# Where a second input piece is issued: SyncE's third load moves to ScalarE's queue, and its transposes are split among the matmuls

## The chip, the cores and the metric

The kernel runs on one core of a Trainium2 chip. The metric is device time in microseconds (us). Three runs of the kernel before gave 117.21, 117.22 and 117.49 us; their median is 117.22 us. A profile is taken in an execution of its own, and its times are counted from the start of its span.

## What is computed

```python
# a: 1024 x 1024, b: 1024 x 2048, c: 2048 x 1024, all float32
h = np.matmul(a, b)
h = 0.5 * h * (1 + np.tanh(np.sqrt(2 / np.pi) * (h + 0.044715 * h ** 3)))
return np.matmul(h, c).astype(np.float32)
```

## The kernel before, in words

TensorE contracts over the partition dimension, so the kernel builds `aT`, the transpose of a in bf16, and computes h transposed: a matmul takes 128 columns of b as weights and 512 columns of `aT` as the moving side. a is handled in eight pieces (h, q): h is the half of its rows (512), q the quarter of its columns (256). A piece becomes two of the eight k-tiles of `aT[:, h]`. b's first 512 columns are loaded in k-tiles of 128 rows; they are multiplied plainly (`mm1`, `block`). The rest of h, and the product with c, is done by class `Seven`, which replaces eight block products by seven and needs sums and differences of blocks on VectorE; that begins at about 24.9 us and is not touched.

The change lies in the first 11 us. What sets the order there:

- **Loads in float32 by SyncE (SP).** `sta` holds pieces of a, `stb` k-tiles of b. Five loads are issued one after the other: a(0,0) at L75, b's k-tiles 0 and 1 at L76 (512 KB, called b0 below), a(1,0) at L77, a(0,1) at L78, b's k-tile 2 at L79. None of them waits for anything.
- **Loads that cast to bf16, by GpSimd (POOL).** Everything else is loaded by GpSimd's queue, straight into `abq` (the five remaining pieces of a, 256 KB each as written), `b1`, `b2` and `c_sb`. The first of them stands behind `gate` (L81), a one-element copy out of a(0,0): no cast-load is issued before a(0,0) has landed. The last piece of a, a(1,3), is the seventh and last of the L86/L89 loads.
- **Casts.** `cast_a` copies a landed piece to bf16 (`ab`), parts of it on VectorE (L110) and ScalarE (L108); `cast_b` does so for a k-tile of b. For a(1,0) VectorE casts the columns of the first k-tile and ScalarE those of the second.
- **Turns.** `turn` is a generator with two steps. Each does four 128 x 128 transposes on TensorE into a PSUM bank (L145) and copies the bank to `aT` on VectorE (L146); `next(tn)` runs one step. Where the steps stand among the matmuls is written out by hand.
- **Matmuls.** `block(h, tiles, ks)` issues, for each k and each tile of 128 columns of b, one matmul of 512 columns (L114).

ScalarE's first instruction is a GELU of one column, `g` (L82). It is there for the table load that it brings, and is called the warm-up. `stir` (L122) gives TensorE work while it waits for the first data.

The stretch that the change edits (L236 to L242) casts b's k-tile 1 and a(1,0), runs four matmuls on k-tile 0 and two on k-tile 1, then both steps of a(1,0)'s turn, then the last two matmuls on k-tile 1. After it come the casts of a(0,1) (L243), three matmuls with a(1,0) (L248) and the turn of a(0,1) (L249), called turn(0,1) below. The turn of the last piece, turn(1,3), stands at L274.

The kernel's functions as they stand before the change:

Of the kernel before, what the change touches and what calls it, by code (L numbers as in the profile page):

```python
# [19 lines left out]
def kernel(ctx, tc, a, b, c, out):  # L20
    nc = tc.nc
    M, K = a.shape
    _, N = b.shape
    _, P = c.shape
# [15 lines left out]
    def slot(tag, shape, dt, name):  # L40
        return big.tile(shape, dt, name=name, tag=tag)

    def bank(i, shape=(128, H), dt=F32, name="ps"):
        return pp.tile(list(shape), dt, name=name, tag=f"bank{i}", padded_shape=None)
# [21 lines left out]
    sta = slot("x1", [128, 2, 2, 4, 256], F32, "sta")  # L66
    abq = slot("x3", [128, 4, 2, 4, 256], BF16, "abq")

    def a_part(h, q):
        return av[:, 4 * h:4 * h + 4, ds(q * 256, 256)]  # L70

    def b_part(q):
        return bv[:, 2 * q:2 * q + 2, 0:H]

    nc.sync.dma_start(out=sta[:, 0, 0], in_=a_part(0, 0))  # L75
    nc.sync.dma_start(out=stb[:, 0:2], in_=b_part(0))  # L76
    nc.sync.dma_start(out=sta[:, 1, 0], in_=a_part(1, 0))  # L77
    nc.sync.dma_start(out=sta[:, 0, 1], in_=a_part(0, 1))  # L78
    nc.sync.dma_start(out=stb[:, 2], in_=bv[:, 2, 0:H])  # L79

    nc.gpsimd.tensor_copy(gate, sta[:, 0, 0, 3, 0:1])  # L81
    nc.scalar.activation(g, warm[:, 0:1], AF.Gelu_apprx_tanh)  # L82


    def cast_load_a(h, q):
# [13 lines left out]
    for n in range(2):  # L99
        for k in range(0, KT, 4):  # L100
            nc.gpsimd.dma_start(out=b2[:, k:k + 4, ts(n, H)],
                                in_=bv[:, k:k + 4, ds(1024 + n * H, H)])
# [9 lines left out]
    def mm1(p, t, h, ks):  # L112
        for k in ks:
            nc.tensor.matmul(p, b1[:, k, ts(t, 128)], aT[:, h, k],  # L114
                             start=(k == 0), stop=(k == KT - 1))
# [12 lines left out]
    def cast_a(h, q, *engs):  # L128

        ab = pieces("ab", 2, [128, 4, 256], BF16, "ab")  # L130
        for i, eng in enumerate(engs):
            w = 256 // len(engs)
            for j, e in enumerate(eng if isinstance(eng, tuple) else (eng,)):
                m = slice(2 * j, 2 * j + 2) if isinstance(eng, tuple) else slice(0, 4)
                copy(e, ab[:, m, ts(i, w)], sta[:, h, q][:, m, ts(i, w)])
        return ab

    def turn(h, q, i, ab):

        banks = i if isinstance(i, tuple) else (i,)  # L140
        pts = [bank(x, (128, 2, H), BF16, "pt") for x in banks]
        for n in range(2):
            pt = pts[n % len(pts)]
            for m in range(4):
                nc.tensor.transpose(pt[:, n, ts(m, 128)], ab[:, m, ts(n, 128)], ident)  # L145
            nc.vector.tensor_copy(aT[:, h, 2 * q + n], pt[:, n])  # L146
            yield
# [8 lines left out]
    def block(h, tiles, ks):  # L156
        for k in ks:
            for t in tiles:
                mm1(ps[h, t], t, h, (k,))
# [70 lines left out]
    tn = turn(0, 0, 4, cast_a(0, 0, nc.vector))  # L230
# [5 lines left out]
    cast_b(1, nc.scalar)  # L236
    ab = cast_a(1, 0, nc.vector, nc.scalar)
    block(0, range(4), (0,))
    block(0, range(2), (1,))
    for _ in turn(1, 0, (7, 6), ab):  # L240
        pass
    block(0, range(2, 4), (1,))  # L242
    ab = cast_a(0, 1, (nc.scalar, nc.vector), nc.vector)  # L243
    cast_b(2, nc.scalar, nc.scalar)
    for t in range(3):
# [3 lines left out]
    tn = turn(0, 1, 7, ab)  # L249
# [4 lines left out]
    for q in range(1, 3):  # L254
        k = 2 * q
        block(0, range(4), (k,))
        tn = turn(1, q, 7, abq[:, q, 1])
# [5 lines left out]
        tn = turn(0, q + 1, 7, abq[:, q + 1, 0])  # L263
# [10 lines left out]
    tn = turn(1, 3, 0, abq[:, 3, 1])  # L274
# [213 lines left out]
```

## Time and profile before

| what | value |
|---|---|
| median of three runs | 117.22 us |
| profiled execution: its own time | 117.6 us |
| profiled execution: its span | 115.8 us |
| TensorE busy | 110.7 us (96% of the span) |
| VectorE, ScalarE, GpSimd busy | 90.1, 51.4, 17.3 us |
| granted TensorE clock | 1.0 in the whole span |
| bytes read from HBM, written | 20.97 MB, 4.19 MB |

The 1.8 us between the profiled execution's time and its span lie outside the recorded work. That execution is 0.4 us above the median, so a difference worked out from its rows is added to 117.22 us.

How it is read: TensorE's busy share is near the span everywhere, and the modelled ends of matmuls make it look closer than it is. What the edited stretch is worth is seen in the order of events between 0.7 and 21.7 us: when each load is issued and lands, when the first instruction that needs it starts, and where TensorE's rows leave a gap. In the half-microsecond windows the last two columns are the mean busy share of the 16 DMA engines and the GB/s written; a cast-load writes half of what it reads.

### The profile page before, as it was taken

To read this page: it belongs to the slowest core of one execution; us is meant where nothing else is said; L and a number is where in the kernel's file an instruction comes from. 1 tells how busy PE (TensorE), PEld (TensorE's weight loads), DVE (VectorE), ACT (ScalarE), POOL (GpSimd) and SP (SyncE) were. 2 spreads that over 40 slices of the span, in tenths; PEclk is the share of its full clock that TensorE was granted. 3 is DMA by queue.
4 is the path that set the end of the run, shared out by engine and by line. 5 is a ranking of instruction groups with operands and counts; after the bars stand their busy time and mean duration, and the time that the engine had idled before them with its cause. 6 is when DMAs were issued, how large, how long until landed. Compare 5 with 4: busy or idle time off the path is not lost.

```text
span 115.8 us, 1473 instructions
## 1 busy us (share of the span) xinstructions
PE 110.7 (96%) x544; PEld 77.1 (67%) x550; DVE 90.1 (78%) x108; ACT 51.4 (44%) x86; POOL 17.3 (15%) x29
## 2 busy tenths in 40 slices
PE   7889999999999999999999999999999999999990
PEld 6545555445777447888886444588888888888870
DVE  0247747689999998944789999999999986964581
ACT  5053000799268998066699339700043992000000
POOL 2497754222332000000000000000000000000000
PEclk9999999999999999999999999999999999999999
DMA  3999999999999999998000000070000002004994
GB/s 74 296 381 221 200 199 204 204 207 207 205 210 210 211 212 212 212 210 163 9 0 0 6 0 0 0 272 0 0 0 0 0 0 94 2 27 173 364 358 166
DMA packets 13414, 15.94 MB, mean 138 GB/s; under 512 B 736, under 2 KB 9184, under 8 KB 13408
## 3 DMA queue, kind: packets, MB, share of 16 engines
q0 software_dynamic: 8672, 9.31, 47.6%
q1 hardware_dynamic: 4592, 6.42, 15.7%
q10 hardware_dynamic: 144, 0.13, 0.3%
q8 instruction: 4, 0.07, 0.2%
q14 instruction: 2, 0.02, 0.0%
HBM read 20.97 MB, written 4.19 MB: 217 GB/s over the span
## 4 chain that ended last, share of the span: by engine, by line
PE 79%; DMA 13%; POOL 5%; issue 0%; DVE 0%
PE ps L212 76%; DMA abq<-in_a_dram 10%; DMA sta<-in_a_dram 3%; POOL abq L86 3%; PE ps L114 2%; POOL b L89 1%; POOL gate L81 1%; PE pt L145 1%; POOL b L92 0%; DVE ot L375 0%
## 5 line engine op out<-in xcount | busy, mean ns | idle before, releaser
L212 PE MATMUL ps<-x,s 128*128 128x512 f32 x128 | 29.6, 391 | 0.0
L212 PEld LDWEIGHTS ps<-x,s 128*128 128x128 f32 x128 | 24.0, 188 | 5.1
L212 PE MATMUL ps<-x,x 128*128 128x512 f32 x96 | 22.9, 394 | 0.0
L212 PEld LDWEIGHTS ps<-x,x 128*128 128x128 f32 x96 | 18.0, 188 | 3.9
L114 PE MATMUL ps<-aT,b 128*128 128x512 bf16 x62 | 15.7, 379 | 0.3 <-DVE b L110 0.2
L298 ACT ACTIVATE v<-ps 128x512 f32<-128x512 f32 x10 | 6.0, 598 | 19.1 <-PE ps L212 19.1
L212 PE MATMUL ps<-c_sb,hT 128*128 128x512 bf16 (+2 forms) x78 | 14.1, 336 | 0.1
L212 PE MATMUL ps<-x 128*128 128x512 f32 x56 | 13.2, 393 | 0.0
L212 PEld LDWEIGHTS ps<-x 128*128 128x128 f32 x56 | 10.2, 188 | 2.7 <-ACT u L298 0.4
L212 PEld LDWEIGHTS <-hT 128*128 128x128 bf16 x80 | 7.1, 98 | 7.0 <-issue 0.5
L118 ACT ACTIVATE hT<-ps 128x512 bf16<-128x512 f32 x14 | 7.3, 596 | 9.6 <-PE ps L114 9.6
L118 ACT ACTIVATE hT<-ot 128x512 bf16<-128x512 f32 x18 | 10.4, 623 | 2.1 <-DVE ot L303 2.0
L146 DVE COPY aT<-pt 128x512 bf16<-128x512 bf16 x16 | 6.7, 422 | 5.5 <-PE pt L145 5.4
L212 PE MATMUL ps<-aT,b 128*128 128x512 bf16 x46 | 10.6, 379 | 0.1
L303 DVE TENSOR_TENSOR ot<-ps,u 128x512 f32<-128x512 f32 x10 | 6.7, 688 | 5.2 <-ACT u L298 5.2
L303 DVE TENSOR_TENSOR ot<-ps,v 128x512 f32<-128x512 f32 x10 | 6.7, 688 | 4.9 <-DMA out_dram<-ot 3.9
L170 DVE TENSOR_TENSOR x<-c_sb 128x1024 fp32r<-128x1024 bf16 x8 | 9.2, 1216 | 0.0
L114 PEld LDWEIGHTS <-b 128*128 128x128 bf16 x64 | 5.7, 97 | 4.5 <-DVE b L110 0.3
L212 PEld LDWEIGHTS <-b 128*128 128x128 bf16 x48 | 4.6, 97 | 5.7 <-issue 0.3
L104 POOL DMA_DIRECT2D c_sb<-in_c_dram x8 | 5.6, 703 | 13.4 <-DMA b<-in_b_dram 11.1
L170 DVE TENSOR_TENSOR x<-b 128x1024 fp32r<-128x1024 bf16 (+1 forms) x4 | 7.0, 1751 | 0.6 <-issue 0.6
L298 ACT ACTIVATE u<-ps 128x512 f32<-128x512 f32 x10 | 5.9, 597 | 3.4 <-PE ps L212 3.2
(44 smaller groups left out, 110.7 us busy)
## 6 DMA issues: line engine op xcount, KB each, us to landing
c_sb<-in_c_dram POOLq DMA_DIRECT2D x8, 512.0 KB, 19.7
out_dram<-ot SPq DMA_DIRECT2D x14, 256.0 KB, 2.1
b<-in_b_dram POOLq DMA_DIRECT2D x6, 512.0 KB, 15.6
sta<-in_a_dram SPq DMA_DIRECT2D x3, 512.0 KB, 6.2
abq<-in_a_dram POOLq DMA_DIRECT2D x5, 256.0 KB, 8.0
stb<-in_b_dram SPq DMA_DIRECT2D x1, 512.0 KB, 5.4
b<-in_b_dram POOLq DMA_DIRECT2D x2, 256.0 KB, 8.3
stb<-in_b_dram SPq DMA_DIRECT2D x1, 256.0 KB, 7.2
```

The source lines that it names most:

```text
L81: nc.gpsimd.tensor_copy(gate, sta[:, 0, 0, 3, 0:1])
L86: nc.gpsimd.dma_start(out=abq[:, q, h], in_=a_part(h, q))
L89: nc.gpsimd.dma_start(out=b1[:, 2 * q:2 * q + 2, 0:H], in_=b_part(q))
L104: nc.gpsimd.dma_start(out=c_sb[:, t:t + 2], in_=cv[:, t:t + 2])
L114: nc.tensor.matmul(p, b1[:, k, ts(t, 128)], aT[:, h, k], start=(k == 0), stop=(k == KT - 1))
L118: nc.scalar.activation(hT[h][:, t], p, AF.Gelu_apprx_tanh)
L145: nc.tensor.transpose(pt[:, n, ts(m, 128)], ab[:, m, ts(n, 128)], ident)
L146: nc.vector.tensor_copy(aT[:, h, 2 * q + n], pt[:, n])
L170: nc.vector.tensor_tensor(out=dst[:, r], in0=x[:, r], in1=y[:, r], op=op)
L212: nc.tensor.matmul(p[:, ds(c0, w)], l[:, k, ts(j, 128)], r[:, k, ds(c0, w)], start=(start and k == 0), stop=(k == self.kt - 1), skip_group ...
L298: nc.scalar.activation(st, p, AF.Copy)
L303: nc.vector.tensor_tensor(out=ot, in0=p, in1=st, op=ADD)
```

## The change

The load of a(1,0) is taken out of SyncE's list and issued from ScalarE's queue, after the warm-up in program order; it has no wait. SyncE's two later loads move up one place. On TensorE, one matmul of k-tile 1 stands ahead of the first step of a(1,0)'s turn instead of two ahead of the whole turn; two follow the first step, and one the second. No instruction is added or removed on any engine.

```diff
     nc.sync.dma_start(out=sta[:, 0, 0], in_=a_part(0, 0))
     nc.sync.dma_start(out=stb[:, 0:2], in_=b_part(0))
-    nc.sync.dma_start(out=sta[:, 1, 0], in_=a_part(1, 0))
     nc.sync.dma_start(out=sta[:, 0, 1], in_=a_part(0, 1))
     nc.sync.dma_start(out=stb[:, 2], in_=bv[:, 2, 0:H])
 
     nc.gpsimd.tensor_copy(gate, sta[:, 0, 0, 3, 0:1])
     nc.scalar.activation(g, warm[:, 0:1], AF.Gelu_apprx_tanh)
+    nc.scalar.dma_start(out=sta[:, 1, 0], in_=a_part(1, 0))
...
     block(0, range(4), (0,))
-    block(0, range(2), (1,))
-    for _ in turn(1, 0, (7, 6), ab):
-        pass
-    block(0, range(2, 4), (1,))
+    block(0, (0,), (1,))
+    tn = turn(1, 0, (7, 6), ab)
+    next(tn)
+    block(0, (1, 2), (1,))
+    next(tn)
+    block(0, (3,), (1,))
     ab = cast_a(0, 1, (nc.scalar, nc.vector), nc.vector)
```

## The prediction

> **What bounds the kernel now.** I read three views in this order: the chain of work that ended last, the timeline of the first 22 us, and half-microsecond windows over the same stretch. The chain first:
>
> ```profile
> 27 pieces in order of time: start us, us, what
> ...
> 0.74 3.70 DMA sta<-in_a_dram
> 4.44 0.05 issue
> 4.49 0.70 POOL gate L81
> ...
> 10.15 11.43 DMA abq<-in_a_dram
> 21.58 0.05 issue
> 21.63 0.40 PE pt L145 x4
> ```
>
> From 21.63 on the chain is TensorE alone, so the end moves one for one with the start of turn(1,3). Two things meet there: the landing of a(1,3) at 21.58, and TensorE itself. The timeline (start, duration, engine, line, operation; what the idle time ended on stands in brackets):
>
> ```profile
> 0.74 0.42 SPq L75 DMA_DIRECT2D sta<-in_a_dram  x1
> 0.74 1.28 ACT L82 ACT_TABLE_LOAD   x1 [0.74 <-PEq L472]
> ...
> 1.22 0.50 SPq L76 DMA_DIRECT2D stb<-in_b_dram  x1
> 1.77 0.46 SPq L77 DMA_DIRECT2D sta<-in_a_dram  x1
> 2.04 0.20 ACT L82 ACTIVATE g<-const-float32-0.0 128x1 f32<-128x1 f32 x1
> ...
> 6.90 1.47 PE L114 MATMUL ps<-aT,b 128*128 128x512 bf16 x6 [0.17 <-DVE b L110]
> ...
> 7.99 0.43 DVE L110 CAST ab<-sta 128x512 bf16<-128x512 f32 x1 [0.68 <-DMA sta<-in_a_dram]
> ...
> 8.47 0.62 PE L145 MATMUL pt<-ident,ab 128*128 128x128 bf16 x8
> ...
> 10.03 0.39 PE L145 MATMUL pt<-ident,ab 128*128 128x128 bf16 x4
> ...
> 19.16 2.32 PE L114 MATMUL ps<-aT,b 128*128 128x512 bf16 x10
> ```
>
> The ten matmuls from 19.16 give the pitch: (2.32 - 0.38) / 9 = 0.215 us, 0.38 being the length of one. TensorE would be ready for turn(1,3) at 19.16 + 10 x 0.215 = 21.31 and starts at 21.63: its **slack is 0.32 us**. Four transposes cost 0.22 (12.02 to the matmul at 12.24). From 10.03 to 21.31 the rows follow at these pitches, so a delay before 10.03 passes through, less 0.32.
>
> The landing at 21.58 is softer than it looks. In the trace's semaphore events fifteen of the sixteen DMA engines had finished a(1,3) by 19.92 and one at 21.58; the packets of the instruction queue (q8 on the page) show a 16 KB packet that starts at 19.57 and takes 0.97 us. I read this as an instruction fetch that came in front of that engine's last packets. Such packets start at 19.57, 40.92, 66.49 and 96.05, 202 to 265 TensorE rows apart, so I take it to follow TensorE's progress. If TensorE is later by over 0.1 us, the fetch should come behind a(1,3), which lands near 20.0, and TensorE alone decides. If TensorE is earlier, the fetch still hits, and an earlier turn(1,3) needs an earlier stream.
>
> **The edit of the order.** After the change TensorE has, from its first real matmul to turn(0,1), 4 + 1 + 2 + 1 + 3 = 11 matmuls and eight transposes: 11 x 0.215 + 2 x 0.22 = 2.81 us if nothing is missing. Before, the same work took 10.03 - 6.90 = 3.13, because a(1,0), landing at 7.97, let the transposes begin at 8.47 only. With unchanged landings the new order is slightly worse: five matmuls end at 7.98 instead of six at 8.19, both before 8.47, so one more stands behind (0.215), and VectorE's copy of the second step (0.42) with the first cast of a(0,1) (0.28) then follow transposes that end near 9.5: turn(0,1) at 10.3, +0.27. That lies within the slack: 21.31 + 0.27 = 21.58 against 21.63. So the order by itself costs nothing; without the slack it would cost 0.27.
>
> **The moved load.** What ScalarE's queue does with a DMA behind an ACTIVATE has no row; two bounds do. Late: after `g`, 2.04 + 0.20 = 2.24. Early: as soon as the queue can pass it, at about 0.85 behind the table load's start at 0.74. I take early. The trace shows ScalarE's sequencer passing the semaphore waits of L202 at 21.09, before the third and fourth GELU ahead of it (21.41, 21.89) have started, and `g` starts 0.01 after the table load ends, as if already queued. Nothing else stands behind this issue (0.42 to 0.71 by SyncE's five rows) on ScalarE until the cast at 6.62.
>
> SyncE's a(0,1) and b's k-tile 2 are issued 0.5 us sooner (one issue with its gap); they lie behind b0 in the same queue, so that buys nothing while the engines are full. GpSimd's queue is moved past nothing, but its gate waits for a(0,0). Then the bytes:
>
> ```profile
> 4.00:4.50 0.50, 0.50 (x4) 0.35 (x2) 0.04 (x1) 0.00 (x0) 0.01 (x1) 1.00 1.19 303
> 4.50:5.00 0.50, 0.29 (x2) 0.00 (x0) 0.50 (x1) 0.00 (x0) 0.50 (x1) 1.00 0.75 221
> 5.00:5.50 0.50, 0.29 (x5) 0.29 (x5) 0.15 (x1) 0.00 (x0) 0.50 (x2) 1.00 0.85 233
> ...
> 7.00:7.50 0.50, 0.50 (x3) 0.29 (x3) 0.31 (x1) 0.50 (x2) 0.50 (x2) 1.00 1.10 387
> ```
>
> The last two columns are the DMA engines' share and GB/s. Full rate is near 387. Adding the windows up, a(0,0)'s 0.524 MB are through at 3.80 (landing 4.44), b0's at 5.71 (landing 6.62, 0.9 later), a(1,0)'s at 7.15 (landing 7.97). The engines are never idle for long, so a(1,0) can only come earlier by taking bytes from a(0,0) and b0, or by filling the dip between 4.0 and 5.75.
>
> Issued early, a(1,0) runs beside a(0,0). Both are through between 5.08 (0.250 MB at 3.0, the rest at 385) and 5.71 (when the first two loads were before). b0 follows: 1.36 us at full rate, 1.91 if its dip moves with it, but no later than 7.15, when the same three loads were through. So b0 lands between 5.08 + 1.36 + 0.9 = 7.34 and 7.15 + 0.9 = 8.05, against 6.62. I take the middle, 7.7, since either end rests on one of two readings of the dip. First matmul 0.28 after the landing as now (6.62 to 6.90): 7.98; turn(0,1) at 7.98 + 2.81 = 10.79, +0.76; less the slack, **+0.44 us**. The ends give +0.08 (7.34) and +0.79 (8.05). a(0,0), landing near 5.6, puts its own turn about 1.1 us later, under the longer wait for b0.
>
> The Trainium skill speaks against the move: "DMA: Bandwidth & Descriptors", section "Issuing engines are not separate DMA queues", says that DMAs of all issuing engines end on the same 16 engines and only the sequencer's issue time is saved. By that rule alone the gain would be the 0.5 us of issue time, hidden, so nothing. The same page, section "Queues, rings and completion order", has each engine take turns between queue rows packet by packet. By that, b0 is pushed back as above; no row here shows two such hardware queues sharing for long, and GpSimd's queue beside SyncE's speaks otherwise, as the second rival says.
>
> **Rivals.**
>
> 1. *The gate becomes the wall.* a(0,0) lands 1.0 to 1.2 us later, and with it GpSimd's issues. Before, they begin at 5.14 and their first packet runs at 8.82 in the trace, just as SyncE's loads run out. If those 3.7 us are latency and not a wait for free engines, the whole cast stream shifts by about 1.0, and so does a(1,3): 118.2. For it: nothing is written by that queue before 8.8. Against: it starts on each engine just when SyncE's packets end there.
> 2. *a(1,0) is served last.* If an engine empties SyncE's queue before another's, as that start at 8.82 suggests, a(1,0) lands at about 9.4, where the four other loads end. Its transposes start 0.5 later at 9.9, turn(0,1) comes after two steps and six matmuls (0.44 + 1.29) at 11.63: +1.60, less 0.32 is +1.28, so 118.5.
> 3. *The other side: the issue is late and fills the dip.* If the DMA does wait for `g`, it is issued at 2.24 and its packets come 1.1 later (0.74 to the first packet at 1.83), at 3.3, when a(0,0) is nearly through. What b0 leaves free between 4.0 and 5.75, (387 - 265) x 1.75 = 0.21 MB or up to 0.5 us, carries a(1,0), which then lands near 7.6 with b0 still near 6.6. First step at 8.08 (cast, as now, 0.5 after landing), turn(0,1) near 9.85 (-0.18), and the stream behind is 0.4 earlier, a(1,3) at 21.2: -0.4, 116.8. It decides if b0 lands before 6.9.
> 4. *It does not do what it says.* The load is taken in the old place between b0 and a(0,1): only the order is left, 117.2.
>
> **How the numbers follow.** About 0.3% (0.35 us) is what a measurement of this kernel can tell from no change. Forecast, 0.44 chance: 117.22 + 0.44 = 117.66, own range 117.3 to 118.0; of it 0.31 beyond 0.35 us and 0.13 within. Gate 0.12, all slower. Served last 0.10, slower. Late and filling 0.22: 0.18 faster, 0.04 within. No effect 0.12, within. Slower 0.53, within 0.29, faster 0.18. The range leaves out rival 2 and the outermost of rival 3: 116.75 to 118.3.
>
> **What would show it.** Right: the issue row of a(1,0) starts before 1.3 with the warm-up still running; a(0,0) lands after 5.2, b0 between 7.3 and 8.1 and not far from a(1,0); first L114 matmul near 8.0, turn(0,1) near 10.8; a(1,3) lands near 20 with no wait ahead of turn(1,3). Wrong: an issue row at 2.2 or later; b0 at 6.6; GpSimd's loads landing a microsecond later with TensorE waiting for `abq`; a wait on a(1,0) before its transposes.

## The result, and the profile after

Eleven runs of the kernel before, taken beside those of the changed one, have a median of 117.33 us; the changed kernel's eleven have 118.70 (117.74 to 119.88). The ratio is 1.0077, 95% interval 1.0050 to 1.0105: slower by 0.9 us. In four of the eleven the mean granted TensorE clock was 0.982 to 0.986; the ratio leaves them out. The forecast was slower, by 0.44 us.

The profiled execution of the changed kernel took 118.7 us with a span of 116.9. Its timeline (start, duration, engine, line, operation, what the idle time ended on):

```profile
0.74 1.28 ACT L81 ACT_TABLE_LOAD   x1 [0.74 <-PEq L474]
...
0.74 0.44 SPq L75 DMA_DIRECT2D sta<-in_a_dram  x1
...
0.80 0.46 ACTq L82 DMA_DIRECT2D sta<-in_a_dram  x1
...
5.18 0.69 DVE L110 CAST ab<-sta 128x1024 bf16<-128x1024 f32 x1 [5.18 <-DMA sta<-in_a_dram]
...
7.66 1.50 PE L114 MATMUL ps<-aT,b 128*128 128x512 bf16 x5 [0.21 <-DVE b L110]
...
10.77 0.38 PE L145 MATMUL pt<-ident,ab 128*128 128x128 bf16 x4
...
13.51 1.04 PE L114 MATMUL ps<-aT,b 128*128 128x512 bf16 x4 [0.38 <-DMA b<-in_b_dram]
...
17.48 0.23 PEld L145 LDWEIGHTS <-abq 128*128 128x128 bf16 x4 [0.50 <-DMA abq<-in_a_dram]
...
22.79 0.39 PE L145 MATMUL pt<-ident,abq 128*128 128x128 bf16 x4
```

The load behind the warm-up does not stand behind it: it is issued at 0.80, while the table load runs. VectorE's first cast starts at 5.18 instead of 4.46, the first matmul on data at 7.66 instead of 6.90, turn(0,1) at 10.77 instead of 10.03. That is 0.72 to 0.76, once. It begins with the order of the packets: b0's first packet runs at 5.00 instead of 3.66, now that a(1,0)'s packets run beside a(0,0)'s and ahead of it, and from there to its landing b0 takes 2.36 us instead of 2.93. Then comes a wait at 13.51 for b's k-tile 3, a cast-load. The kernel before runs the same four matmuls without one:

```profile
12.24 1.03 PE L114 MATMUL ps<-aT,b 128*128 128x512 bf16 x4
```

A second wait, for `abq` at 17.48, grew by 0.20 us (the kernel before has 0.30 there). So turn(1,3) starts at 22.79 instead of 21.63. The chain of waits now runs through that load:

```profile
39 pieces in order of time: start us, us, what
...
5.91 0.81 POOL abq L86
6.72 6.74 DMA b<-in_b_dram
13.47 0.05 issue
13.51 1.04 PE ps L114 x4
```

The windows of the changed kernel at those times (last two columns: share of the DMA engines, GB/s written):

```profile
3.50:4.00 0.50, 0.50 (x3) 0.41 (x2) 0.00 (x0) 0.00 (x0) 0.00 (x0) 1.00 1.09 389
4.00:4.50 0.50, 0.50 (x3) 0.41 (x2) 0.00 (x0) 0.00 (x0) 0.00 (x0) 1.00 1.03 362
...
10.00:10.50 0.50, 0.50 (x4) 0.20 (x2) 0.42 (x2) 0.15 (x1) 0.50 (x2) 1.00 1.47 130
10.50:11.00 0.50, 0.50 (x7) 0.33 (x6) 0.50 (x2) 0.00 (x0) 0.50 (x2) 1.00 0.78 87
11.00:11.50 0.50, 0.50 (x6) 0.26 (x4) 0.48 (x2) 0.00 (x0) 0.50 (x1) 1.00 0.98 73
```

and of the kernel before at two of them:

```profile
10.50:11.00 0.50, 0.50 (x5) 0.23 (x4) 0.38 (x1) 0.32 (x2) 0.48 (x1) 1.00 1.33 205
11.00:11.50 0.50, 0.45 (x6) 0.35 (x6) 0.14 (x1) 0.00 (x0) 0.00 (x0) 1.00 1.32 195
```

From 10 to 12 the cast stream of the changed kernel runs at 73 to 130 GB/s where it ran at about 200. In the trace's packets the reads of k-tile 3 took 96 to 1044 ns in that stretch instead of 96 to 98, and its sixteen parts land between 11.00 and 13.47 (before: 11.29 to 11.98). Some reads of a among them were slow too (mean 204 ns from 11.0 to 11.5, where 60 is usual). This is called the stall below. It is measured by how long after a(1,1), the cast-load ahead of it, k-tile 3 lands: 2.78 us instead of 0.64.

### The profile page after: what moved, and what is told of

Same layout as the page of the kernel before. It is cut to its first block, busy times and chain, and to the rows that moved or that the text cites. A ratio compares the mean times of both kernels' runs of the same rounds, so it can differ in the third digit from the quotient of the medians.

```text
span 116.9 us, 1473 instructions
## 1 busy us (share of the span) xinstructions
PE 111.1 (95%) x544; PEld 77.3 (66%) x550; DVE 89.9 (77%) x108; ACT 51.3 (44%) x86; POOL 17.2 (15%) x29
## 4 chain that ended last, share of the span: by engine, by line
PE 86%; DMA 10%; POOL 1%; issue 0%; DVE 0%
PE ps L212 75%; PE ps L114 9%; DMA b<-in_b_dram 6%; DMA sta<-in_a_dram 4%; PE pt L145 2%; POOL abq L86 1%; POOL gate L80 1%; DVE ot L377 0%
## 5 line engine op out<-in xcount | busy, mean ns | idle before, releaser
L212 PE MATMUL ps<-x 128*128 128x512 f32 x56 | 13.2, 392 | 0.0
L118 ACT ACTIVATE hT<-ot 128x512 bf16<-128x512 f32 x18 | 10.6, 625 | 1.8 <-DVE ot L305 1.7
L212 PE MATMUL ps<-aT,b 128*128 128x512 bf16 x46 | 10.6, 379 | 0.1
```

Source lines behind the costliest of these rows:

```text
L118: nc.scalar.activation(hT[h][:, t], p, AF.Gelu_apprx_tanh)
L212: nc.tensor.matmul(p[:, ds(c0, w)], l[:, k, ts(j, 128)], r[:, k, ds(c0, w)], start=(start and k == 0), stop=(k == self.kt - 1), skip_group ...
```

## The experiments

Theory A (shared start): two hardware queues share the engines from the start, so b0, the third load, is late, and TensorE with it. Theory B: the new order of turns carries the loss. Theory C asks whether the stall in the cast stream belongs to the change (C1) or is chance (C2); later its cause is sought in GpSimd's later issue (G) or in the second hardware queue (Q).

Landings (the last of sixteen parts) are from the semaphore events, starts from the timeline, us; "b0 first" is the start of b0's first packet, and behind k-tile 3's landing stands how long after a(1,1) it came. The ratio has its 95% interval.

| kernel | a(0,0) | a(1,0) | b0 first | b0 | k-tile 3 | first matmul | turn(0,1) | turn(1,3) | span | ratio |
|---|---|---|---|---|---|---|---|---|---|---|
| before | 4.44 | 7.97 | 3.66 | 6.59 | 11.98 (+0.64) | 6.90 | 10.03 | 21.63 | 115.8 | 1 |
| changed | 5.16 | 5.63 | 5.00 | 7.36 | 13.47 (+2.78) | 7.66 | 10.77 | 22.79 | 116.9 | 1.0077 (1.0050-1.0105) |
| order_only | 4.24 | 7.86 | 3.41 | 6.49 | 11.88 (+0.65) | 6.81 | 10.15 | 21.43 | 115.6 | 1.0026 (1.0007-1.0045) |
| move_only | 5.20 | 5.67 | 4.90 | 7.22 | 12.84 (+2.28) | 7.53 | 10.39 | 22.09 | 116.2 | 1.0125 (1.0088-1.0162) |
| late | 4.29 | 10.06 | 3.46 | 6.41 | 12.55 (+1.25) | 6.77 | 12.43 | 23.72 | 117.8 | 1.0202 (1.0183-1.0222) |
| swap | 6.71 | 8.06 | 2.50 | 6.44 | 13.22 (+1.72) | 9.41 | 14.12 | 25.41 | 119.5 | 1.0239 (1.0168-1.0310) |
| before_gate2 | 4.10 | 7.90 | 3.41 | 6.54 | 11.94 (+0.71) | 6.92 | 9.97 | 21.26 | 115.4 | 0.9995 (0.9955-1.0035) |
| after_timed | 5.17 | 5.65 | 4.97 | 7.56 | 11.94 (+0.70) | 7.87 | 10.91 | 22.21 | 116.4 | 1.0079 (1.0037-1.0120) |
| after_b3first | 5.11 | 5.58 | 4.88 | 7.27 | 10.50 (ahead of it) | 7.58 | 10.44 | 21.73 | 115.9 | 1.0057 (1.0011-1.0103) |
| before_later | 4.25 | 8.81 | 3.39 | 7.22 | 13.11 (+0.96) | 7.53 | 10.88 | 22.43 | 116.6 | 1.0075 (1.0047-1.0103) |
| after_earlier | 5.29 | 5.76 | 5.01 | 7.30 | 12.58 (+1.66) | 7.71 | 10.57 | 21.90 | 116.1 | 1.0089 (1.0050-1.0129) |
| one_queue | 4.23 | 6.26 | 4.94 | 9.53 | 13.56 (+0.68) | 10.10 | 14.61 | 25.90 | 120.0 | 1.0352 (1.0313-1.0392) |
| after_stir | 5.28 | 5.76 | 5.01 | 7.54 | 13.07 (+2.19) | 7.85 | 10.90 | 22.40 | 116.6 | 1.0094 (1.0072-1.0116) |

The span is the start of turn(1,3) plus 94.1 to 94.2 us in every row. So all that these profiles differ by within the span happens before it. Where a(1,0) is issued at 0.80 from ScalarE's queue, b0's first packet runs at 4.88 to 5.01; with the old loads and in late it runs at 3.39 to 3.66.

**after_again**: the changed kernel once more, no edit.

> The changed kernel once more. Theory A (shared start): ScalarE's issue starts near 0.8, a(0,0) lands near 5.2, b0 near 7.4, first L114 matmul near 7.7, as in the first profile. Theory C1 (the stall in the cast stream belongs to the change): b's k-tile 3 lands near 13.5 again and TensorE waits about 0.4 us for it near 13.5; ratio 1.007 to 1.011. Theory C2 (the stall is chance): k-tile 3 lands near 12 as before the change, no such wait, turn(1,3) about 0.8 later than in the kernel before instead of 1.2, and a time nearer 1.004.

Measured: ratio 1.0083 (1.0047 to 1.0119). The issue was at 0.80 again; a(0,0) landed at 5.09, b0 at 7.42, k-tile 3 at 13.17. Its profiled execution fell to half the clock at 8.08 for 3.4 us, so only its landings are read. A holds, and C2 is out: the stall is there again (k-tile 3 came 2.40 us after a(1,1)).

**order_only**: the loads of before, the new order of turns.

```diff
+    nc.sync.dma_start(out=sta[:, 1, 0], in_=a_part(1, 0))
...
-    nc.scalar.dma_start(out=sta[:, 1, 0], in_=a_part(1, 0))
```

> Loads as before the change, only the turn of a(1,0) split among the matmuls. Theory A: turn(0,1) at 10.2 to 10.3 instead of 10.03, hidden by the slack of 0.32 us ahead of turn(1,3); ratio 0.998 to 1.001. Theory B (the order carries the loss): turn(0,1) later than 10.6 and a ratio over 1.004.

Measured: 1.0026, or 0.30 us of 117.25 (0.08 to 0.53). turn(0,1) came at 10.15 with a first matmul at 6.81: 3.34 us for the stretch, against 3.13 and 3.05 in the two profiles of the old order (before, before_gate2). B falls, as its 10.6 was not reached; but the expected cover was not there either. In this profile

```profile
21.43 0.39 PE L145 MATMUL pt<-ident,abq 128*128 128x128 bf16 x4
```

stands without a wait: a(1,3) had landed at 19.84.

**move_only**: the moved load, the old order (the diff's first two hunks alone).

> The load moved to ScalarE's queue, the old order of turns and matmuls. Theory A: b0 near 7.4, first matmul near 7.7, turn(0,1) near 10.5 to 10.7 as after the change; ratio 1.004 to 1.010, not to be told from the whole change. Theory B: at or below 1.002. Theory C1: b's k-tile 3 late again, near 13.5; C2: near 12.

Measured: b0 7.22, first matmul 7.53, k-tile 3 at 12.84 with a wait of 0.30 for it:

```profile
12.89 0.55 PEld L114 LDWEIGHTS <-b 128*128 128x128 bf16 x4 [0.30 <-DMA b<-in_b_dram]
```

The ratio of 1.0125 lies a little above the expected range, and its interval overlaps the whole change's. The move alone is enough for the loss: A and C1.

**late**: the warm-up writes where the load will land, so that the load waits for it.

```diff
-    nc.scalar.activation(g, warm[:, 0:1], AF.Gelu_apprx_tanh)
+    nc.scalar.activation(sta[:, 1, 0, 0, 0:1], warm[:, 0:1], AF.Gelu_apprx_tanh)
```

> As the changed kernel, but the warm-up writes into one element of a(1,0)'s place, so that the load has to wait for it (the load then overwrites it). Theory A, with engines taking turns packet by packet: issue near 2.3, first packet near 3.4, a(0,0) at 4.5 as before, b0 (packets twice as long) at 6.6 to 6.9, a(1,0) at 7.6 to 8.0, first matmul 6.9 to 7.2, ratio 0.997 to 1.002. If taking turns costs b0 half the rate from 3.8 on: b0 at 7.3 or later and a ratio over 1.003.

Measured: both expectations missed. The load was issued at 2.26, but its first packet ran at 6.02, not 3.4, and most came after 6.75; it landed last, at 10.06, and b0 kept its 6.41. TensorE stood before the transposes:

```profile
2.26 0.45 ACTq L82 DMA_DIRECT2D sta<-in_a_dram  x1
...
6.77 1.24 PE L114 MATMUL ps<-aT,b 128*128 128x512 bf16 x5
...
10.65 0.40 PE L145 MATMUL pt<-ident,ab 128*128 128x128 bf16 x4 [2.64 <-DVE ab L110]
```

The late queue's packets came in only behind those of the other: 1118 of SyncE's had run by 6.75, some 70 for each of the sixteen engines, and 22 of ScalarE's. From 7.0 on the packets alternate (92 of ScalarE's and 84 of SyncE's in the next half microsecond). I read this as waiting behind what each engine already held; the trace shows the order of the packets and not that reason.

**swap**: b0 on ScalarE's queue beside a(0,0), a(1,0) second on SyncE's.

```diff
-    nc.sync.dma_start(out=stb[:, 0:2], in_=b_part(0))
+    nc.sync.dma_start(out=sta[:, 1, 0], in_=a_part(1, 0))
...
-    nc.scalar.dma_start(out=sta[:, 1, 0], in_=a_part(1, 0))
+    nc.scalar.dma_start(out=stb[:, 0:2], in_=b_part(0))
```

> The order of turns as after the change, but it is b0 that ScalarE's queue issues beside a(0,0), and a(1,0) stays on SyncE's queue right behind a(0,0). Theory A (the two queues share the engines packet by packet, so whoever is third of the three is late): a(0,0) lands near 5.0, b0 near 5.5, a(1,0) near 7.2; first matmul 6.9 to 7.1, limited by the casts, no wait for a(1,0); turn(0,1) at 9.8 to 10.0. If the stall in the cast stream comes with two queues (C1), k-tile 3 lands after 12.5 and the ratio is 1.000 to 1.006; without the stall 0.996 to 1.001.

Measured: 1.0239, far outside. b0's packets, slow in the other profiles too (84 ns is usual; here up to 514), now ran beside a(0,0)'s, and a(0,0) landed at 6.71 only. TensorE idled from 5.4 to 7.5, and its matmuls of 9.41 to 13.2 took 634 ns at a pitch of 0.427 us instead of 0.215: half the clock. That the idling did this is not shown, for the filler ran at that pitch from the start:

```profile
0.78 4.61 PE L125 MATMUL ps<-const-float32-0.0 128*128 128x256 f32 x10 [0.78 <-PEq L474]
```

The trace's clock records begin at 13.20 in this execution, and the clock column reads 1.00 where there is no record. In the kernel before they begin at 4.04, and the filler speeds up there (0.427 to 0.22 us apart), so the "1.0 in the whole span" of its table holds from 4.04 on. Of the 4.15 us by which swap's turn(0,1) is behind before_gate2's, 2.49 stand at the first matmul; the other 1.66 come behind it, in the stretch at half the clock. Giving b0 the second queue did not beat the old order.

**before_gate2**: the gate's copy twice, in the kernel before.

```diff
+    nc.gpsimd.tensor_copy(gate, sta[:, 0, 0, 3, 1:2])
```

> The kernel before with a second one-element copy in the gate, so that GpSimd issues its first load near 5.85, as it does in the changed kernel, and everything else as before. Rival 1 (the gate is the wall): the cast stream and a(1,3) shift by 0.7, ratio 1.004 or more. If the cast stream waits for free engines: first packet at 8.8 as before, same landings, ratio 0.998 to 1.002. If the stall in the cast stream comes of GpSimd issuing later: k-tile 3 lands after 12.5 here too.

Measured: the second copy took 0.18 us, and GpSimd's first load was issued at 5.04, not 5.85. It tests nothing of the gate. It serves as the profile of an ordinary execution of the old order instead: 117.19 us, and

```profile
21.26 0.39 PE L146 MATMUL pt<-ident,abq 128*128 128x128 bf16 x4
```

with a(1,3) landed at 19.89. A 16 KB instruction packet ran from 19.67 here too, and a(1,3) was not late.

**after_timed**: the gate replaced by five copies of a constant.

```diff
-    nc.gpsimd.tensor_copy(gate, sta[:, 0, 0, 3, 0:1])
+    for _ in range(5):
+        nc.gpsimd.tensor_copy(gate, warm[:, 0:1])
```

> The changed kernel with a gate that does not look at a(0,0): five one-element copies of a constant, so that GpSimd issues its first load near 5.0, as in the kernel before. If the later gate brings the stall: k-tile 3 lands near 12 and the ratio falls to 1.002 to 1.005. If the stall comes with the two hardware queues: k-tile 3 after 12.5 again, ratio as the changed kernel, 1.007 to 1.011.

Measured: the copies are short, and the first issue came at 2.35. Its first packet ran at 7.27, and from 7.5 on it shared the engines with SyncE's loads (82 to 89 packets of GpSimd's and 82 to 84 of SyncE's in each half microsecond from 8.0 to 9.5). k-tile 3 came at 11.94 without slow packets, but a(0,1) only at 10.33. The stall is gone, and the ratio is not better: in this profile b0 landed at 7.56 and the first matmul came at 7.87, 0.95 behind before_gate2's, and that is all of the distance at turn(1,3) (22.21 against 21.26). Why b0 is later here than in the other profiles with the moved load (7.22 to 7.54) was not tried.

**after_b3first**: in the changed kernel, k-tile 3 as the first cast load.

```diff
-    cast_load_a(1, 1)
     nc.gpsimd.dma_start(out=b1[:, 3, 0:H], in_=bv[:, 3, 0:H])
+    cast_load_a(1, 1)
```

> The changed kernel with b's k-tile 3 as the first cast load and a(1,1) as the second. If the stall belongs to the reading of that k-tile: its packets are slow again, near 9, it lands by 11.5 with 5 to 8 engines late, and TensorE does not wait for it but for a(1,1). If it belongs to the moment (10 to 12 us): k-tile 3 lands near 10.2 with engines close together, and a(1,1) is the late one. In both cases the wait near 13.5 for k-tile 3 is gone; ratio 1.004 to 1.010.

Measured: k-tile 3 landed at 10.50, its packets only mildly slow (mean 108 ns), and the pieces of a read between 10 and 12 were not slow (means of 60 and 61 ns): in this one profile the moment alone brings no stall. No wait is left between

```profile
7.58 1.25 PE L114 MATMUL ps<-aT,b 128*128 128x512 bf16 x5 [0.18 <-DVE b L110]
...
10.44 0.38 PE L145 MATMUL pt<-ident,ab 128*128 128x128 bf16 x4
...
21.73 0.39 PE L145 MATMUL pt<-ident,abq 128*128 128x128 bf16 x4
```

What remains, 21.73 against 21.26 in before_gate2, is b0's delay alone: 0.47 us here. The ratio is 1.0057.

**before_later**: four more copies behind the gate of the kernel before.

```diff
+    for _ in range(4):
+        nc.gpsimd.tensor_copy(gate, warm[:, 0:1])
```

> The kernel before with four more one-element copies behind the gate, so that GpSimd issues its first load at 5.7 to 6.0, as in the changed kernel; the loads of the other queues as before the change. Theory G (the stall comes of GpSimd issuing late, with one hardware queue too): b's k-tile 3 lands after 12.5 with packets over 150 ns between 10 and 12, TensorE waits for it, ratio 1.003 to 1.008. Theory Q (the stall needs the second hardware queue): k-tile 3 lands at 11.9 to 12.0, ratio 0.998 to 1.002.

Measured: issue at 5.93, k-tile 3 at 13.11, ratio 1.0075. The landing and the ratio are what G expected, but not by G's mechanism. The whole stream is late here: a(1,1) landed at 12.15, and k-tile 3 came 0.96 after it, against 0.64 to 0.71 with the old loads and 2.19 to 2.78 in the changed kernel. So its reads are somewhat slow without a second hardware queue (means of 102 to 190 ns in half microseconds), but a stall of the changed kernel's size is not there, and Q stands. TensorE's delay begins with b0 (landed 7.22, first matmul 7.53), whose packets are slow before the first added copy at 5.07. b0's first packet runs at 3.39, so this late b0 is a slow read and not theory A's late start; so that b0 lands after 7 is by itself no proof of A; that its first packet comes late is. Why added copies on GpSimd go with it is open.

**after_earlier**: sixteen copies of a constant as the gate of the changed kernel (as after_timed, 16 for 5).

> The changed kernel with sixteen one-element copies of a constant as the gate, so that GpSimd issues its first load near 5.0, as in the kernel before, but not as early as 2.35, where it pushed SyncE's loads back. Theory G: no stall, k-tile 3 lands near 12, turn(1,3) starts near 22.1, ratio 1.003 to 1.006. Theory Q: k-tile 3 after 12.5, a wait for it near 13.5, ratio 1.007 to 1.011.

Measured: issue at 5.04; k-tile 3 at 12.58, 1.66 after a(1,1), so the stall is there with GpSimd's old issue time and G falls; but it came soon enough that TensorE did not wait for it; turn(1,3) at 21.90. In this profile turn(1,3) is 0.64 behind before_gate2's and the first matmul 0.79: b0's delay is all of it. The ratio, 1.0089, is the changed kernel's, but it misleads: this kernel's times lie 1.97 to 2.10 us above their spans, all others' 1.72 to 1.85, so some 0.27 us of its loss are outside the profiled work, for a reason not sought. Seven of its ten runs have spans of 115.9 to 116.1 and three 117.5 to 117.8; the kernel before has a median of 115.5, and the changed kernel, low clocks aside, goes from 115.8 to 117.3 with a median of 116.5. So within the span the earlier issue seems to win back a part of the loss; how much these runs do not settle.

**one_queue**: a(1,0) second on SyncE's own queue, nothing on ScalarE's, the new order.

```diff
     nc.sync.dma_start(out=sta[:, 0, 0], in_=a_part(0, 0))
+    nc.sync.dma_start(out=sta[:, 1, 0], in_=a_part(1, 0))
     nc.sync.dma_start(out=stb[:, 0:2], in_=b_part(0))
...
-    nc.scalar.dma_start(out=sta[:, 1, 0], in_=a_part(1, 0))
```

> The order of turns as after the change, but a(1,0) on SyncE's queue, second, between a(0,0) and b0; nothing on ScalarE's. Theory A in its parts: a(0,0) lands on time, near 4.4, a(1,0) near 5.8, b0 third at 7.2 to 7.9 as after the change; first matmul 7.5 to 8.2, turn(0,1) 10.4 to 11.0. The sharing by itself (a(0,0) late) then costs nothing on TensorE's path. GpSimd issues near 5.1: theories G and Q both expect no stall; ratio 1.002 to 1.007.

Measured: 1.0352. a(0,0) was on time and b0 third, as expected, but b0 landed at 9.53: between 5 and 6.25 its packets took 125 to 451 ns in the mean of each quarter microsecond, and the windows show

```profile
5.50:6.00 0.50, 0.26 (x4) 0.09 (x3) 0.36 (x1) 0.00 (x0) 0.50 (x2) 1.00 0.40 92
```

From its first packet (4.94) to its landing b0 took 4.59 us; in the kernel before it took 2.93. TensorE had nothing for 3.6 us, and its clock (the third column from the right) fell after that:

```profile
9.50:10.00 0.50, 0.00 (x0) 0.00 (x0) 0.44 (x2) 0.45 (x2) 0.50 (x2) 1.00 1.23 314
10.50:11.00 0.50, 0.50 (x3) 0.18 (x2) 0.50 (x1) 0.50 (x2) 0.26 (x1) 0.59 1.32 231
11.50:12.00 0.50, 0.50 (x5) 0.23 (x3) 0.00 (x0) 0.23 (x1) 0.00 (x0) 0.50 1.41 201
```

It returned at 14.0. Of the 4.64 us by which turn(0,1) is behind before_gate2's, 3.18 stand at the first matmul, and 1.46 come in the stretch with the low clock. b0's first packet runs as late as in the changed kernel, so being third in line gives the late start with or without the second queue; the slow read that follows is a second loss, and its cause is open. What sharing costs by itself this run does not tell.

**after_stir**: the changed kernel with longer filling work on TensorE.

```diff
-    stir(256, 256, 256, 256, 256)
+    stir(256, 256, 256, 256, 256, 256, 128)
...
-    stir(128)
+    stir(256)
...
-    stir(64)
+    stir(256)
```

> The changed kernel with TensorE's filling work lengthened (1.6 us more of it in the three places where it waits for a(0,0), for the copy and for b0; the added work is thrown away). What is asked: runs of the changed kernel whose mean granted clock was 0.982 to 0.986, and about 1.5 us longer, came in 5 of 18. If TensorE's idling between 4.6 and 7.7 us lets the clock fall, none of some ten runs should lie under 0.99 here. If they are chance, some two or three of ten. The first matmul on data stays at 7.6 to 7.8 either way, and the ratio of the undisturbed runs at 1.006 to 1.011: no theory expects the filling to win back b0's delay.

Measured: 1.0094; no run of six lies under 0.997 of the clock. With 5 in 18 as the rate, six such runs in a row would come by chance in 14% of cases; with the four other kernels that have the load at 0.80 (4 in 36) counted in, in a third. So it does not settle the cause. For idling speaks that means under 0.99 are most frequent where TensorE stands still longest: four of four in one_queue, three of four in swap, three of six in late, against one in 74 runs of the kernel before. b0's delay stays, as expected.

## Why the prediction was right, and where it was wrong

The way was right, and so was the main mechanism: a(1,0) shares the engines with a(0,0), and b0 starts late. The size was not: 0.44 us were forecast and 0.90 measured, 117.22 x 1.0077 = 118.12, which is above the forecast's own 117.3 to 118.0 and inside the whole range.

- **The issue.** Right: 0.85 was taken, 0.80 measured, with the table load still running. ScalarE's sequencer did not hold this DMA, which has no wait, behind the ACTIVATE ahead of it.
- **Sharing.** Right. In the trace's packets from 3.0 to 4.5, SyncE's a(0,0) and ScalarE's a(1,0) run 41 to 48 packets each in every quarter microsecond. This agrees with what "DMA: Bandwidth & Descriptors", section "Queues, rings and completion order", in the Trainium skill says of queue rows taking turns. In late and after_timed the queue that was issued later ran its first packet 3.8 and 4.9 us after its issue, and only then did the packets alternate.
- **b0.** The mechanism was right: its first packet came 1.34 us later. It landed at 7.36, at the early end of the 7.34 to 8.05 given, not at 7.7. The dip became milder, so the stream ran at 389 and 362 GB/s in the two halves of 3.5 to 4.5, and b0's own read was faster (2.36 us for 2.93).
- **From the first matmul to turn(0,1).** 2.81 us were forecast, 3.11 measured. The order needs VectorE in a stretch that I priced by TensorE alone: its two casts of b took 0.68 us where they took 0.36, and TensorE's second weights came at 8.12. With the same order and load it took 2.86 in after_b3first and after_earlier and 3.04 in after_timed and after_stir, so a part of the 0.30 is this execution's alone. b0's earlier landing and this cancel, which is luck: turn(0,1) was put at 10.79 and came at 10.77.
- **The slack of 0.32 us.** This step failed. It was read from an execution of 117.6 us, in which a(1,3) landed at 21.58, and then subtracted from a sum that was added to the median, 117.22. An execution at the median has no such wait: before_gate2 starts turn(1,3) at 21.26. The cover was counted twice, once by the median and once by the sum. Without it the forecast is 117.22 + 0.76 = 117.98. order_only shows the same term: 0.27 was called hidden, and 0.30 us were measured. That the instruction packet was what held a(1,3) back is a reading that no other profile repeats: in before_gate2 and order_only such packets ran from 19.67 and 19.61, and a(1,3) landed whole at 19.89 and 19.84.
- **The stall of k-tile 3.** Not foreseen. From turn(0,1) to turn(1,3) before_gate2 needs 11.29 us; the changed kernel's profile needs 12.02, 0.73 more. 0.80 (10.77 against 9.97) and 0.73 make 1.53, about the difference of the spans, 116.9 against 115.4. By the ratio the loss is 0.9, and the spans that it rests on go from 115.9 to 117.0, so I take it that the share of the stall varies; after_earlier and after_b3first have none of it in turn(1,3), and both are still slower.
- **The instruction fetch.** Read rightly as bound to TensorE's progress: in thirteen of the fourteen profiles it starts 1.5 to 2.1 us ahead of turn(1,3) (after_stir, with more TensorE work ahead: 2.8). In the changed kernel it came at 21.14, and nothing waited ahead of turn(1,3). That a(1,3) would land near 20 was wrong (21.39), because the stall had moved the stream.
- **Rival 1, the gate.** Its mechanism falls: GpSimd's issue moved from 5.14 to 5.86 and its first packet from 8.82 to 8.66. Its prediction that the cast stream would come about a microsecond late, with TensorE waiting for it, came true for another reason, and its 118.2 is the nearest to the 118.12 measured. Such waits were also named as a sign of being wrong, and that sign came.
- **Rivals 2 to 4.** Served last is not what the change does, but it is what late does: 1.0202. Rival 3 held that a late issue fills the dip; late issued at 2.26, and a(1,0) came last, at 10.06. Rival 4 is out by the landings.

What stays open is why reads stall. b0's are slow in every profile that was read packet by packet (before, changed, swap, late, one_queue, before_later, after_timed), and reads of a are at times (before, 2.0 to 2.5: mean 125 ns where 46 is usual). Of the eight profiles that have a load on ScalarE's queue and take k-tile 3 second among the cast loads, seven have the stall (1.25 to 2.78 us behind a(1,1)), and after_timed has not (0.70). The five without one have 0.64 to 0.96. So the stall goes with the second hardware queue, Q's side, and not with GpSimd's issue time (late 4.98 and after_earlier 5.04 have it, if shorter than the changed kernel); how the one brings the other is not shown, and after_timed speaks against a simple rule. Which addresses of a and b lie how in memory was not tried.

## What to carry to other kernels

A load on an idle queue is not free bandwidth: name the load that it pushes back, and ask what starts with that one. A late landing does not say why: look whether the first packet came late or the packets ran slowly. Read a slack from an execution at the median, or add the sum to the execution that it was read from. And find the last point to which everything before it can be reduced: here the start of one transpose gave the span of all these kernels to within 0.1 us.

## What the runs showed of the hardware

- A DMA issue on ScalarE's queue overtook a table load and an ACTIVATE (issued 0.80, the ACTIVATE ran at 2.03). With a real dependence on the ACTIVATE it was held (late: 2.26).
- A read of the same 512 KB took from 2.29 us (after_earlier) to 4.59 us (one_queue), from its first packet to its landing; the kernels differ in what was loaded before and beside it.
- In the kernel before the last sixteenth of a(1,3) landed 1.66 us after the others (19.92, 21.58), with an instruction packet of 16 KB running from 19.57 for 0.97 us. Whether the packet did it is not shown.
- After 3.6 us without work TensorE's granted clock went to 0.50 at 10.59 and came back at 14.01 (one_queue): 3.4 us. "TensorE: Matmul & The Clock Gate" in the Trainium skill, section "What's actually happening", states a window of about 3.4 us for both directions. In after_again the clock was also down for 3.4 us (8.08 to 11.49), but TensorE had not stood still for more than 0.77 us at a time before, so a whole window without work was not needed there.
- The profile's clock column reads 1.00 where the trace has no clock record. In swap the records begin at 13.20, and every matmul before ran at half rate (those of 512 columns 0.427 us apart instead of 0.215).
